# The step from 32 to 64 rows of a block inverse on 64-column weights, and a new order of the instructions

## The chip, the cores and the metric

One core of one Trainium2 chip. The metric is the device time of one execution of the kernel in microseconds (us); lower is better. The kernel before takes 2718.01 us, the median of three runs (2717.71, 2718.01 and 2719.68).

## The reference

One decoder layer on 2048 tokens of width 1024. Its first half joins a gated DeltaNet mixer (8 heads of width 128, chunks of 64 tokens) with a cross-attention of 4 heads to 256 memory rows; an output projection, a layer norm, a squared-ReLU MLP (1024 to 4096 to 1024) and a second layer norm follow. What the change touches is the triangular solve of the DeltaNet: for every head and every chunk

```
a_mat = eye(64) + strict_lower((k * beta) @ k.T * decay)
u = solve(a_mat, v * beta)
w = solve(a_mat, k * beta * exp(g))
```

The kernel takes chunks of 128 tokens for the 64 of the reference, which gives the same result; it computes the inverse of each 128x128 `a_mat` and multiplies by it.

## The kernel before, in words

**Blocks and heads.** The tokens are taken in four blocks of 512. In the mixer of a block a loop of ten steps (`mixer`) runs three stages of a software pipeline over the heads: `dense` projects q, k and v of head t (24 matmuls each), `gdn_a` builds the decayed products of head t-1, inverts them (`invert`) and scales the rest, `gdn_b` runs the recurrence of head t-2 over its four 128-token tiles. Gate projections (`az`), memory projections and attention (`amq`, `sps`, `pmT`, `pmo`) fill further places of the steps. After two blocks come the output projection (`out_seven`, tile `ao`) and the two MLP products (`ff1`, `ff2`; `fA` to `fC` and `f2A` to `f2C`), each as seven products of half-size operands. All of it happens twice.

**Two kinds of matmuls.** Large products run on operands split into a high and a low part of type float32r; each matmul on these is one record of the profile, with 128 weight columns and mostly 512 moving ones. This text calls them f32r. The inverse, the recurrence, some of the key products (`pkq`, four heads), the gates' first product (`aab`) and the transposes have float32 operands; a matmul on these makes two records of the profile and a transpose one. This text calls them f32. The profile prints f32 for both, so they are told apart by the tile's name.

**The inverse** (`invert`, lines 889 to 1007) works on one head's four 128-token tiles at a time; each product on TensorE takes them two by two (index c). Blocks of 16 rows are solved on VectorE. Then three steps double the size, 16 to 32, 32 to 64 and 64 to 128, each with the same form: product `pq` of a part of the lower triangle, copy from PSUM, product `pp` with the inverse so far, copy from PSUM with the sign turned. Each product is two matmuls (c = 0, 1), so four records. The middle step is this:

```
pq = bank("pq", ...)[:, :64]                       # L32: 128 weight columns, ZP: 32 moving
for c in range(2): nc.tensor.matmul(pq[:, c], L32[:, c], ZP[:, c] ...)
nc.scalar.copy(out=Q[:, 64:P] ..., in_=pq)
for c in range(2): nc.tensor.matmul(pp[:, c], X32[:, c], Q[:, 64 + c * 32:...])
```

There are 4 blocks x 8 heads = 32 inversions. The tiles XB, LB, L32, X32, X64, LP and Q stand in four slots (`INV`, `inverse_tiles`) that are set to zero once for every two blocks; ZP lies in the first half of `Lq`, the negated result and its transpose in the second half and in the first again.

**The order.** Nothing is issued while the Python code runs. `Recorder` notes every instruction with an estimate of its time (`cost`); `issue` then plays a list schedule: whenever an engine is free, it takes, of the instructions whose operands are ready by the estimate, the one with the lowest priority number. That number is the place in the program, shifted by a table (`PLACE`, read by `spot`) keyed by block, step and stage: B for `gdn_b`, A for `gdn_a`, D for `dense`, Z for the gates, F for a panel of `ff1`, X and W for the operands of `out_seven`, and so on. The order covers all engines, with SP's DMA issues among them, and is written out with fixed semaphores; on the chip each engine works through its own list in that order. All instructions are issued at line 431 (`o.fn`), which is why the profile shows one line; groups are told apart by tiles. In the schedule of before a change in the number of weight columns can be given a cost (`SWITCH`), which is 0.

`gate_rows` is of use for the prediction: it multiplies 32-column weights (`abw`) on 512 moving columns, float32, into the four quarters of `aab`'s partitions. `gates` holds the transpose `pgt`, whose result has 32 partitions.

Of the kernel before, what the change touches and what calls it, by code (L numbers as in the profile page):

```python
# [14 lines left out]
P = 128  # L15
# [20 lines left out]
DRAIN, SWITCH = {"DVE": 90, "ACT": 100, "POOL": 98}, 0  # L36
# [148 lines left out]
class Op:  # L185
    __slots__ = ("i", "eng", "fn", "args", "kw", "dur", "extra", "succ", "npred", "ready", "start", "end", "load", "last",
                 "bufs", "turns", "prio", "quads", "cols", "late", "lhs")
# [21 lines left out]
class Recorder:  # L209
# [66 lines left out]
    @staticmethod  # L276
    def cost(o, name, wr, rd, args, kw):
        e = o.eng
        shapes = [r.shape for r in wr] + [r.shape for r in rd]
        n = max([_prod(s[1:]) for s in shapes] or [1])  # L280
        if e == "PE":
            rhs = kw.get("rhs", args[2])
            mo, n = _prod(args[1].shape[1:]), _prod(rhs.shape[1:])
            f32 = name == "transpose" or isinstance(rhs, Ref) and rhs.buf.dtype == F32
            o.load, o.cols, o.lhs = 4 + 0.84 * mo, mo, args[1].buf if isinstance(args[1], Ref) else None
            o.last = 2.4 + 0.8334 * n if f32 else 13.4 + 0.4167 * n
            if name == "transpose":
                return o.last
            if f32 and mo == 32 and n == 512:
                return (o.last + max(o.last, o.load)) / 4  # L290
            if f32:
                return o.last + max(o.last, o.load)
            return o.last
        psum = any(r.buf.psum for r in rd + wr)
        if e == "SP":
            n = _prod(wr[0].shape if wr else rd[0].shape)
            o.extra = 1700 + n * 4 / 300.0
            o.late = 2000 if rd and any(s[0] == "partition_broadcast" for s in rd[0].steps) else 300
            return 450
        scal = [v for v in args[2:] if not isinstance(v, (int, float))] if name.startswith("tensor_scalar") else []  # L300
        scal += [v for k, v in kw.items() if k in ("scalar", "scalar1", "scale", "bias") and not isinstance(v, (int, float))]
        if e == "ACT":
            n = _prod((wr[0]).shape[1:])
            return 52 + 0.833 * n + (0 if psum else 42) + 93 * len(scal) + ((305 if scal else 198) if "accum_out" in kw else 0)
        if e == "DVE":
            slow = 30 if name in ("transpose", "stream_shuffle") else 0
            fast = not psum and not any(r.perm() for r in rd + wr) and name in ("tensor_copy", "tensor_scalar_mul", "tensor_scalar_add", "tensor_scalar_max",
                                         "memset")
            return 68 + slow + (0.52 if fast else 1.042) * n + 62 * len(scal) + (7 * n if name == "reciprocal" else 0)
        if name == "memset":  # L310
            return 40 + 0.83 * n
        if kw.get("op") == ALU.pow:
            return 460 + 165 * n
        if name == "tensor_copy":
            return 120 + 0.83 * n
        if name == "affine_select":
            return 125 + 0.9 * n
        return 150 + (2.1 if n < 64 else 2.8) * n if name == "tensor_tensor" else 296 + 3.34 * n

    def issue(self):  # L320
# [7 lines left out]
        quads, cols = {e: {} for e in DRAIN}, P  # L328
# [42 lines left out]
        while True:  # L371
# [3 lines left out]
            for e in engs:  # L375
                if avail[e]:
# [10 lines left out]
            while soon[e] and soon[e][0][0] <= t:  # L387
                r, i, o = heapq.heappop(soon[e])
                heapq.heappush(avail[e], (o.prio, i, o))
            o = heapq.heappop(avail[e])[2]  # L390
            if e == "PE":
                if o.cols != cols:
                    t += SWITCH
                    cols = o.cols
                t = max(t, fed + o.load)
                fed = t + o.dur - o.last
            if e in DRAIN:
# [4 lines left out]
            o.start, o.end = t, t + o.dur  # L402
# [45 lines left out]
def hybrid_layer(  # L448
# [91 lines left out]
    for h in range(H):  # L540
# [7 lines left out]
    INV = (("XB", (2, P)), ("LB", (2, P)), ("L32", (2, P)), ("X32", (2, P)), ("X64", (2, P)),  # L548
           ("LP", (2, P)), ("Q", (2 * P,)))

    def inverse_tiles():
        d = {}
        for i in range(0, len(INV), 2):
            t = slot("inv", "iv")
            nc.gpsimd.memset(t, 0.0)
            for j, (n, shape) in enumerate(INV[i:i + 2]):
                v = t[:, j * 2 * P:(j + 1) * 2 * P]
                d[n] = v if len(shape) == 1 else v.rearrange("p (u f) -> p u f", u=2)
# [330 lines left out]
    def invert(L, par):  # L889
# [8 lines left out]
        for p in range(2):  # L898
            rows = slice(64 * p + 32, 64 * p + 64)
            nc.gpsimd.tensor_copy(L32[rows, :, 64 * p:64 * p + 32].part((0, p)), L[rows, 0:2, 64 * p:64 * p + 32])  # L900
            nc.vector.tensor_copy(L32[64 * p:64 * p + 32, :, 64 * p + 32:64 * p + 64].part((1, p)),
# [28 lines left out]
        XB, LB, X32, X64, Q = (inv[n] for n in ("XB", "LB", "X32", "X64", "Q"))  # L930
# [13 lines left out]
        Q16 = Q[:, :64].rearrange("p (u f) -> p u f", u=2)  # L944
# [4 lines left out]
        for c in range(2):  # L949
            nc.tensor.matmul(pp[:, c * 32:(c + 1) * 32], XB[:, c, :W], Q[:, c * 32:(c + 1) * 32].part(0, 3),  # L950
# [5 lines left out]
        ZP = Lq.rearrange("p c f -> p (c f)")[:, :64].rearrange("p (c f) -> p c f", c=2)  # L956
        Z = small("Z32", [P, NC, 32], 2)
        for p in range(2):
            odd = slice(64 * p + 32, 64 * p + 64)
            nc.vector.tensor_copy(ZP[64 * p:64 * p + 32].part(2 * p + 1), ZT[odd, 2:4])  # L960
            nc.scalar.copy(out=ZP[odd].part(2 * p), in_=ZT[odd, 0:2])
        nc.vector.transpose(Z.rearrange("p c f -> p (c f)"), ZT.rearrange("p c f -> p (c f)"))
        for p in range(2):
            for u in range(2):
                q = quads[2 * p + u]
                nc.vector.tensor_copy(X32[q, :, q].part((u, p)), Z[64 * p:64 * p + 32, 2 * u:2 * u + 2])
# [7 lines left out]
        pq = bank("pq", "ga%d" % par)[:, :64].rearrange("p (c f) -> p c f", c=2)  # L974
        for c in range(2):
            nc.tensor.matmul(pq[:, c], L32[:, c], ZP[:, c].part(0, 1, 2, 3), start=True, stop=True)
        nc.scalar.copy(out=Q[:, 64:P].rearrange("p (c f) -> p c f", c=2).part(1), in_=pq)
        pb = bank("pp", "ga%d" % par)[:, :64]
        pp = pb.rearrange("p (c f) -> p c f", c=2)
        for c in range(2):  # L980
            nc.tensor.matmul(pp[:, c], X32[:, c], Q[:, 64 + c * 32:64 + (c + 1) * 32].part(1), start=True, stop=True)
        Nf = Lq.rearrange("p c f -> p (c f)")[:, 64:]
        nc.scalar.activation(Nf, pb, AF.Copy, scale=-1.0)
        tr = Lq.rearrange("p c f -> p (c f)")[:64, :64]
        nc.vector.transpose(tr, Nf[:64])
        N3 = Nf.rearrange("p (c f) -> p c f", c=2)
        for p in (1, 0):
            o = Y3[64 * p:64 * p + 32, :, 64 * p + 32:64 * p + 64]
            nc.vector.tensor_copy(o[:, 2:4], N3[quads[2 * p + 1]])
            nc.scalar.copy(out=o[:, 0:2], in_=N3[quads[2 * p]])  # L990
        tr = tr.rearrange("p (c f) -> p c f", c=2)
        for u in range(2):
            nc.vector.tensor_copy(X64[quads[2 * u + 1], :, quads[2 * u]].part((u, 2)), tr[quads[u]])
# [7 lines left out]
        nc.scalar.copy(out=Q[:, P:].rearrange("p (c f) -> p c f", c=2).part(2), in_=pq)  # L1001
        pp = bank("pp", "ga%d" % par)[:, :P].rearrange("p (c f) -> p c f", c=2)
        for c in range(2):
            nc.tensor.matmul(pp[:, c], X64[:, c], Q[:, P + c * 64:P + (c + 1) * 64].part(2), start=True, stop=True)
# [912 lines left out]
```

## Time and profile before

| | before |
|---|---|
| median of 3 runs | 2718.01 us (2717.71 to 2719.68) |
| span of the profiled execution | 2718.7 us |
| TensorE busy | 2702.6 us (99%), 13625 records |
| VectorE busy | 2097.3 us (77%) |
| ScalarE busy | 1627.0 us (60%) |
| GpSimd busy | 403.6 us (15%) |
| mean granted TensorE clock | 0.999 |

The profile gives no time of the profiled execution apart from its span, from the first to the last instruction; it lies 0.7 us above the median and within the three runs. PE stands for matmuls, PEld for weight loads. Records of matmuls overlap, since each lasts until its last result is written, so what one costs is read from the start of one to the start of the next. In the timeline neighbouring instructions of one kind are merged into one row: start, length to the end of the last, engine, tiles, weight rows*columns, moving shape, number of records.

### The profile page before, as it was taken

What the parts mean: (1) busy time and instruction counts of PE and PEld (TensorE: products, weight loads), DVE (VectorE), ACT (ScalarE), POOL (GpSimd) and SP (SyncE); (2) the same over time, 40 slices, a digit from 0 to 9 for tenths busy, and PEclk for the clock granted to TensorE, in tenths of its full rate; (3) what the DMA queues carried; (4) which work ended last, traced back from release to release, by engine and by line L of the source; (5) the groups of instructions that cost most, each with busy time, mean ns of one, the idle gap of its engine ahead of it and who ended that gap; (6) DMA issues with size and microseconds to landing.
All of it is one profiled execution on the core that took longest, in us unless ns stands there. A gap on an engine that the chain in (4) does not pass through costs nothing.

```text
span 2718.7 us, 42521 instructions
## 1 busy us (share of the span) xinstructions
PE 2702.6 (99%) x13625; PEld 2264.0 (83%) x13625; DVE 2097.3 (77%) x5652; ACT 1627.0 (60%) x4106; POOL 403.6 (15%) x1031
## 2 busy tenths in 40 slices
PE   9999999999999999999999999999999999999998
PEld 7888888888888888888888888888888888888887
DVE  7999989998877776755767888788878666567575
ACT  7778767776575555334446776677656655554342
POOL 4233223331000000000022231332201000000000
PEclk9999999999999999999999999999999999999999
DMA  8766649867788888766663445444678644486673
GB/s 315 253 232 210 213 170 321 293 240 261 278 315 286 297 294 298 264 212 197 231 226 136 171 137 186 156 152 157 226 260 295 220 164 141 158 283 221 214 238 112
DMA packets 209072, 613.81 MB, mean 226 GB/s; under 512 B 24112, under 2 KB 32720, under 8 KB 188880
## 3 DMA queue, kind: packets, MB, share of 16 engines
q1 hardware_dynamic: 208416, 611.04, 64.7%
q8 instruction: 108, 1.77, 0.3%
q14 instruction: 116, 0.95, 0.1%
q10 hardware_dynamic: 432, 0.05, 0.0%
HBM read 436.35 MB, written 174.65 MB: 225 GB/s over the span
## 4 chain that ended last, share of the span: by engine, by line
PE 94%; DVE 2%; ACT 2%; DMA 1%; POOL 1%; issue 0%; SPq 0%; DVEq 0%; ACTq 0%; POOLq 0%
PE f2A L431 13%; PE fA L431 13%; PE ao L431 8%; PE fC L431 6%; PE f2C L431 6%; PE az L431 6%; PE aq L431 6%; PE av L431 6%; PE ak L431 6%; PE amq L431 3%; PE fB L431 3%; PE f2B L431 3%; PE pc L431 3%; PE po L431 2%; PE pkq L431 2%; PE pq L431 1%
## 5 line engine op out<-in xcount | busy, mean ns | idle before, releaser
L431 DVE TENSOR_TENSOR whl<-wraw,whl 128x512 fp32r<-128x512 f32 (+2 forms) x294 | 256.5, 883 | 109.8 <-ACT whl L431 107.9
L431 ACT CAST whl<-wraw 128x512 fp32r<-128x512 f32 (+2 forms) x294 | 226.4, 781 | 164.4 <-PE fC L431 54.5
L431 PE MATMUL fA<-B,whl 128*128 128x512 f32 x1152 | 279.1, 389 | 0.0
L431 PE MATMUL f2A<-whl,X 128*128 128x512 f32 x1152 | 262.1, 389 | 0.0
L431 ACT CAST X<-X 128x1024 fp32r<-128x1024 f32 x118 | 124.0, 1052 | 223.3 <-DMA X<-xsc 183.3
L431 PEld LDWEIGHTS fA<-B,whl 128*128 128x128 f32 x1152 | 216.2, 188 | 45.1
L431 PEld LDWEIGHTS f2A<-whl,X 128*128 128x128 f32 x1152 | 216.2, 188 | 44.9
L431 DVE TENSOR_TENSOR X<-X,X 128x1024 fp32r<-128x1024 f32 x118 | 143.8, 1221 | 126.0 <-ACT X L431 125.9
L431 PE MATMUL az<-T,whl 128*128 128x512 f32 x768 | 218.5, 406 | 0.0
L431 PE MATMUL aq<-T,whl 128*128 128x512 f32 x768 | 215.6, 406 | 1.7 <-DVE whl L431 0.8
L431 PE MATMUL ak<-T,whl 128*128 128x512 f32 x768 | 214.8, 407 | 0.1
L431 PE MATMUL av<-T,whl 128*128 128x512 f32 x768 | 209.1, 402 | 0.0
L431 PE MATMUL fC<-B,whl 128*128 128x512 f32 x768 | 192.3, 389 | 0.0
L431 PE MATMUL f2C<-whl,X 128*128 128x512 f32 x768 | 174.7, 389 | 0.0
L431 PEld LDWEIGHTS fC<-B,whl 128*128 128x128 f32 x768 | 144.1, 188 | 30.0
L431 PEld LDWEIGHTS f2C<-whl,X 128*128 128x128 f32 x768 | 144.1, 188 | 29.9
L431 PEld LDWEIGHTS aq<-T,whl 128*128 128x128 f32 x768 | 137.5, 189 | 27.4 <-DVE T L431 2.0
L431 PEld LDWEIGHTS av<-T,whl 128*128 128x128 f32 x768 | 138.5, 189 | 24.3
L431 PEld LDWEIGHTS ak<-T,whl 128*128 128x128 f32 x768 | 135.8, 189 | 22.3 <-ACT whl L431 0.4
L431 PEld LDWEIGHTS az<-T,whl 128*128 128x128 f32 x768 | 136.4, 189 | 21.2
L431 POOL TENSOR_SCALAR ve<-mv 128x1 f32<-128x1 f32 x34 | 15.3, 451 | 912.2 <-DVE mv L431 906.0
L431 PE MATMUL ao<-whl,X 128*128 128x512 f32 x528 | 136.8, 401 | 0.0
(294 smaller groups left out, 6292.2 us busy)
## 6 DMA issues: line engine op xcount, KB each, us to landing
whl<-wsc SPq DMA_DIRECT2D x108, 1024.0 KB, 4.9
wraw<-in_w_ff_dram SPq DMA_DIRECT2D x106, 512.0 KB, 4.3
X<-xsc SPq DMA_DIRECT2D x96, 512.0 KB, 4.1
wsc<-whl SPq DMA_DIRECT2D x36, 1024.0 KB, 6.4
whl<-tsc SPq DMA_DIRECT2D x64, 512.0 KB, 4.8
xsc<-hB SPq DMA_DIRECT2D x96, 256.0 KB, 2.5
xo<-cat SPq DMA_DIRECT2D x80, 256.0 KB, 4.1
wraw<-in_w_in_dram SPq DMA_DIRECT2D x35, 512.0 KB, 6.5
```

The source lines that it names most:

```text
L431: o.fn(*[res(a) for a in o.args], **{k: res(v) for k, v in o.kw.items()})
```

## The change

Part one is the middle step of the inverse. The blocks of the weights of `pq` and `pp` are moved together, so that they have 64 columns where they had 128 (L32 and X32 become 2 x 64), and the moving operands have 64 columns where they had 32 (new tiles Z64 and Q64 with zeros in half their places). The result stands on 64 partitions. Its sign is turned once, 32 rows of it are transposed, and one copy on each of VectorE and ScalarE puts it into Y where there were two. Z64, Q64, N and NT have places of their own in the four slots of the inverse's tiles.

Part two is the order. Each matmul is marked `wide` if it is f32, and TensorE gets two heaps of ready work. After f32 work it stays with f32 work if that has a priority number below that of the f32r work plus 200 (`STAY`); after fewer than five f32r matmuls it goes back only to f32 work whose number is lower by more than 300 (`LEAVE`, `RUN`); otherwise the lower number wins. The schedule's estimate adds 5 ns on entering f32 work and up to 8 ns to each of the first ten f32r matmuls behind it. The table PLACE is replaced by a longer one.

```diff
-DRAIN, SWITCH = {"DVE": 90, "ACT": 100, "POOL": 98}, 0
+DRAIN = {"DVE": 90, "ACT": 100, "POOL": 98}
+INTO, AFTER = 5, (8, 4, 6, 6, 0, 4, 5.5, 1.5, 4, 2.5)
+STAY, LEAVE, RUN = 200, 300, 4
...
 PLACE = {
-    ('w',): 140, (0, 0, 'H'): -305, (0, 1, 'D'): -225, (0, 1, 'H'): -435, (0, 1, 'Y'): -145, (0, 1, 'Z'): -165,
...
+    (None,): -90, ('w',): 135, (0, 0, 'D'): 255, (0, 0, 'F'): -420, (0, 0, 'H'): -300, (0, 1, 'A'): 185,
...
             f32 = name == "transpose" or isinstance(rhs, Ref) and rhs.buf.dtype == F32
+            o.wide = f32 or not isinstance(rhs, Ref)
...
-                heapq.heappush(avail[e], (o.prio, i, o))
-            o = heapq.heappop(avail[e])[2]
+                heapq.heappush(wide if e == "PE" and o.wide else avail[e], (o.prio, i, o))
+            heap = avail[e]
+            if e == "PE" and wide:
+                if not heap:
+                    heap = wide
+                elif was:
+                    heap = wide if wide[0][0] < heap[0][0] + STAY else heap
+                elif run < RUN:
+                    heap = wide if wide[0][0] < heap[0][0] - LEAVE else heap
+                else:
+                    heap = wide if wide[0][:2] < heap[0][:2] else heap
+            o = heapq.heappop(heap)[2]
...
-    INV = (("XB", (2, P)), ("LB", (2, P)), ("L32", (2, P)), ("X32", (2, P)), ("X64", (2, P)),
-           ("LP", (2, P)), ("Q", (2 * P,)))
+    INV = ((("XB", (2, P)), ("LB", (2, P))), (("X64", (2, P)), ("LP", (2, P))),
+           (("L32", (2, 64)), ("X32", (2, 64)), ("Z64", (2, 64)), ("Q64", (2, 64))),
+           (("Q16", (64,)), ("Q", (P,)), ("N", (NC, 32)), ("NT", (NC, 32))))
...
-        pq = bank("pq", "ga%d" % par)[:, :64].rearrange("p (c f) -> p c f", c=2)
+        pq = bank("pq", "ga%d" % par)[:64, :P].rearrange("p (c f) -> p c f", c=2)
         for c in range(2):
             nc.tensor.matmul(pq[:, c], L32[:, c], ZP[:, c].part(0, 1, 2, 3), start=True, stop=True)
-        nc.scalar.copy(out=Q[:, 64:P].rearrange("p (c f) -> p c f", c=2).part(1), in_=pq)
-        pb = bank("pp", "ga%d" % par)[:, :64]
-        pp = pb.rearrange("p (c f) -> p c f", c=2)
+        for u in range(2):
+            nc.scalar.copy(out=QP[64 * u:64 * u + 64, :, 32 * u:32 * u + 32].part(u), in_=pq[:, :, 32 * u:32 * u + 32])
+        pp = bank("pp", "ga%d" % par)[:64, :P]
         for c in range(2):
-            nc.tensor.matmul(pp[:, c], X32[:, c], Q[:, 64 + c * 32:64 + (c + 1) * 32].part(1), start=True, stop=True)
-        Nf = Lq.rearrange("p c f -> p (c f)")[:, 64:]
-        nc.scalar.activation(Nf, pb, AF.Copy, scale=-1.0)
...
+            nc.tensor.matmul(pp[:, c * 64:(c + 1) * 64], X32[:, c], QP[:, c].part(0, 1), start=True, stop=True)
+        nc.scalar.activation(N3[:64].rearrange("p (u c) f -> p u c f", u=2), pp.rearrange("p (c u f) -> p u c f", c=2, u=2),
+                             AF.Copy, scale=-1.0)
+        nc.vector.transpose(NT[:32].rearrange("p c f -> p (c f)"), N3[:32].rearrange("p c f -> p (c f)"))
+        nc.vector.tensor_copy(Y3[64:96, :, 96:], N3[32:64])
+        nc.scalar.copy(out=Y3[:32, :, 32:64], in_=N3[:32])
```

## Rows read from the trace of the kernel before

**Rows 1.** The page's busy times, and the core's span with its granted clock

```profile
PE 2702.6 (99%) x13625; PEld 2264.0 (83%) x13625; DVE 2097.3 (77%) x5652; ACT 1627.0 (60%) x4106; POOL 403.6 (15%) x1031
...
core 0: 2718.7 us, clock 0.999
```

**Rows 2.** Who PE waited for: total us, times, longest

```profile
PE pt L431 <- ACT st L431: 1.4, 2, 0.9
...
PE pt L431 <- ACT y L431: 0.2, 1, 0.2
```

**Rows 3.** A window of the first MLP: length, then busy us and records per engine

```profile
780.00:1320.00 540.00, 540.00 (x2384) 447.11 (x2383) 381.45 (x526) 267.29 (x387) 6.88 (x14) 1.00 0.78 266
```

**Rows 4.** PE's groups by shape: the middle step's first product

```profile
L431 PE MATMUL pq<-Lq,inv 128*128 128x32 f32 x128 | 17.1, 255 | 0.3 <-POOL inv L431 0.3
```

**Rows 5.** PEld's groups by shape: busy us, mean ns of one load

```profile
L431 PEld LDWEIGHTS pp<-inv 128*128 128x128 f32 x256 | 36.8, 190 | 5.9 <-issue 0.9 <-ACT inv L431 0.8 <-POOL halo L431 0.2
...
L431 PEld LDWEIGHTS aab<-xj,abw 128*32 128x32 f32 x64 | 1.5, 108 | 3.1 <-issue 2.7 <-DVE Xc L431 0.4
```

**Rows 6.** PE's timeline in mixers: f32 work between stretches of f32r work

```profile
413.00 0.53 PE L431 MATMUL pp<-inv 128*128 128x32 f32 x4
413.36 3.24 PE L431 MATMUL ak<-T,whl 128*128 128x512 f32 x13
416.44 0.55 PE L431 MATMUL pq<-YP,inv 128*128 128x64 f32 x4
...
564.03 0.56 PE L431 MATMUL pq<-YP,inv 128*128 128x64 f32 x4
564.40 1.18 PE L431 MATMUL ak<-T,whl 128*128 128x512 f32 x4
565.41 0.55 PE L431 MATMUL pp<-inv 128*128 128x64 f32 x4
...
577.20 0.27 PE L431 MATMUL pmT<-ident,pr 128*128 128x128 f32 x1
577.23 0.48 PE L431 MATMUL av<-T,whl 128*128 128x512 f32 x1
577.55 0.38 PE L431 MATMUL pkq<-ck 128*128 128x128 f32 x2
577.76 0.39 PE L431 MATMUL pkq<-cq,ck 128*128 128x128 f32 x2
```

**Rows 7.** The first and the last f32 stretch of PE's timeline

```profile
1.19 4.64 PE L431 MATMUL warm<-ones 128*128 128x128 f32 x20 [1.19 <-POOL mhalf L518]
...
2110.02 0.60 PE L431 MATMUL pt<-ident,y 128*128 128x128 f32 x4
```

**Rows 8.** PE's timeline around matmuls and a transpose on 32-column weights

```profile
303.15 1.06 PE L431 MATMUL aab<-xj,abw 128*32 128x512 f32 x8
304.15 0.73 PE L431 MATMUL sps<-mkv,mq 128*128 128x256 f32 x4
...
1340.28 0.39 PE L431 MATMUL f2A<-whl,xl 128*128 128x512 f32 x1
1340.59 1.92 PE L431 MATMUL aab<-xj,abw 128*32 128x512 f32 x16
1342.45 0.74 PE L431 MATMUL f2A<-whl,xh 128*128 128x512 f32 x2
1343.03 0.40 PE L431 MATMUL f2A<-whl,xl 128*128 128x512 f32 x1
...
1367.11 0.39 PE L431 MATMUL f2A<-whl,xl 128*128 128x512 f32 x1
1367.34 0.27 PE L431 MATMUL pgt<-ident,gc 128*32 128x128 f32 x1
1367.36 0.71 PE L431 MATMUL f2A<-whl,xh 128*128 128x512 f32 x2
1367.91 0.40 PE L431 MATMUL f2A<-whl,xl 128*128 128x512 f32 x1
```

More of the change, by code (lines that the diff above doesn't have):

```diff
@@ L186 @@
     __slots__ = ("i", "eng", "fn", "args", "kw", "dur", "extra", "succ", "npred", "ready", "start", "end", "load", "last",
-                 "bufs", "turns", "prio", "quads", "cols", "late", "lhs")
+                 "bufs", "turns", "prio", "quads", "cols", "late", "lhs", "wide")
 PLACE = {
[15 rows of a table removed]
[35 rows of a table added]
 }
@@ L327, in issue @@
         dma = [0.0]
-        quads, cols = {e: {} for e in DRAIN}, P
+        quads = {e: {} for e in DRAIN}
+        wide, was, run = [], False, len(AFTER)
         slots = {k: [0.0] * v[0].bufs for k, v in self.tags.items()}
@@ L375, in issue @@
             for e in engs:
-                if avail[e]:
+                if avail[e] or e == "PE" and wide:
                     t = free[e]
@@ L388, in issue @@
                 r, i, o = heapq.heappop(soon[e])
-                heapq.heappush(avail[e], (o.prio, i, o))
-            o = heapq.heappop(avail[e])[2]
+                heapq.heappush(wide if e == "PE" and o.wide else avail[e], (o.prio, i, o))
[10 more added lines that the diff above has]
+            o = heapq.heappop(heap)[2]
+            took = o.dur
             if e == "PE":
-                if o.cols != cols:
-                    t += SWITCH
-                    cols = o.cols
                 t = max(t, fed + o.load)
                 fed = t + o.dur - o.last
+                if o.wide:
+                    took += 0 if was else INTO
+                else:
+                    run = 0 if was else run + 1
+                    took += AFTER[run] if run < len(AFTER) else 0
+                was = o.wide
             if e in DRAIN:
@@ L401, in issue @@
                 at.update(o.quads)
-            o.start, o.end = t, t + o.dur
+            o.start, o.end = t, t + took
             free[e] = o.end
@@ L547, in hybrid_layer @@
     nc.gpsimd.memset(halo, 0.0)
-    INV = (("XB", (2, P)), ("LB", (2, P)), ("L32", (2, P)), ("X32", (2, P)), ("X64", (2, P)),
-           ("LP", (2, P)), ("Q", (2 * P,)))
+    INV = ((("XB", (2, P)), ("LB", (2, P))), (("X64", (2, P)), ("LP", (2, P))),
+           (("L32", (2, 64)), ("X32", (2, 64)), ("Z64", (2, 64)), ("Q64", (2, 64))),
+           (("Q16", (64,)), ("Q", (P,)), ("N", (NC, 32)), ("NT", (NC, 32))))
     def inverse_tiles():
         d = {}
-        for i in range(0, len(INV), 2):
+        for names in INV:
             t = slot("inv", "iv")
             nc.gpsimd.memset(t, 0.0)
-            for j, (n, shape) in enumerate(INV[i:i + 2]):
-                v = t[:, j * 2 * P:(j + 1) * 2 * P]
-                d[n] = v if len(shape) == 1 else v.rearrange("p (u f) -> p u f", u=2)
+            at = 0
+            for n, shape in names:
+                v = t[:, at:at + _prod(shape)]
+                at += _prod(shape)
+                d[n] = v if len(shape) == 1 else v.rearrange("p (u f) -> p u f", u=shape[0])
         return d
@@ L899, in invert @@
             rows = slice(64 * p + 32, 64 * p + 64)
-            nc.gpsimd.tensor_copy(L32[rows, :, 64 * p:64 * p + 32].part((0, p)), L[rows, 0:2, 64 * p:64 * p + 32])
-            nc.vector.tensor_copy(L32[64 * p:64 * p + 32, :, 64 * p + 32:64 * p + 64].part((1, p)),
+            nc.gpsimd.tensor_copy(L32[rows, :, 32 * p:32 * p + 32].part((0, p)), L[rows, 0:2, 64 * p:64 * p + 32])
+            nc.vector.tensor_copy(L32[64 * p:64 * p + 32, :, 32 * p:32 * p + 32].part((1, p)),
                                   L[rows, 2:4, 64 * p:64 * p + 32])
@@ L929, in invert @@
         nc.vector.transpose(ZT.rearrange("p c f -> p (c f)"), Z.rearrange("p c f -> p (c f)"))
-        XB, LB, X32, X64, Q = (inv[n] for n in ("XB", "LB", "X32", "X64", "Q"))
+        XB, LB, X32, X64, Q, ZP, QP, N3, NT = (inv[n] for n in ("XB", "LB", "X32", "X64", "Q", "Z64", "Q64", "N", "NT"))
         Y = slot("Y", "s0")
@@ L943, in invert @@
             nc.tensor.matmul(pq[:, c], LB[:, c], ZT[:, c:NC:2, 16:32], start=True, stop=True)
-        Q16 = Q[:, :64].rearrange("p (u f) -> p u f", u=2)
+        Q16 = inv["Q16"].rearrange("p (u f) -> p u f", u=2)
         nc.scalar.activation(Q16[:, :, 0:16].part(0), pq[:, :, 0:16], AF.Copy, scale=half[:, 0:1])
@@ L949, in invert @@
         for c in range(2):
-            nc.tensor.matmul(pp[:, c * 32:(c + 1) * 32], XB[:, c, :W], Q[:, c * 32:(c + 1) * 32].part(0, 3),
+            nc.tensor.matmul(pp[:, c * 32:(c + 1) * 32], XB[:, c, :W], Q16[:, c].part(0, 3),
                              start=True, stop=True)
@@ L953, in invert @@
         nc.vector.tensor_tensor(out=zt, in0=zt, in1=pp.rearrange("p (u k f) -> p u k f", u=2, k=2), op=ALU.subtract)
-        ZP = Lq.rearrange("p c f -> p (c f)")[:, :64].rearrange("p (c f) -> p c f", c=2)
         Z = small("Z32", [P, NC, 32], 2)
@@ L959, in invert @@
             odd = slice(64 * p + 32, 64 * p + 64)
-            nc.vector.tensor_copy(ZP[64 * p:64 * p + 32].part(2 * p + 1), ZT[odd, 2:4])
-            nc.scalar.copy(out=ZP[odd].part(2 * p), in_=ZT[odd, 0:2])
+            nc.vector.tensor_copy(ZP[64 * p:64 * p + 32, :, 32:].part(2 * p + 1), ZT[odd, 2:4])
+            nc.scalar.copy(out=ZP[odd, :, :32].part(2 * p), in_=ZT[odd, 0:2])
         nc.vector.transpose(Z.rearrange("p c f -> p (c f)"), ZT.rearrange("p c f -> p (c f)"))
@@ L964, in invert @@
             for u in range(2):
-                q = quads[2 * p + u]
-                nc.vector.tensor_copy(X32[q, :, q].part((u, p)), Z[64 * p:64 * p + 32, 2 * u:2 * u + 2])
+                nc.vector.tensor_copy(X32[quads[2 * u + p], :, 32 * p:32 * p + 32].part((u, p)),
+                                      Z[64 * p:64 * p + 32, 2 * u:2 * u + 2])
         for p in range(2):
@@ L972, in invert @@
             nc.scalar.copy(out=Y3[r, :, r], in_=ZT[r])
-        pq = bank("pq", "ga%d" % par)[:, :64].rearrange("p (c f) -> p c f", c=2)
+        pq = bank("pq", "ga%d" % par)[:64, :P].rearrange("p (c f) -> p c f", c=2)
         for c in range(2):
             nc.tensor.matmul(pq[:, c], L32[:, c], ZP[:, c].part(0, 1, 2, 3), start=True, stop=True)
-        nc.scalar.copy(out=Q[:, 64:P].rearrange("p (c f) -> p c f", c=2).part(1), in_=pq)
-        pb = bank("pp", "ga%d" % par)[:, :64]
-        pp = pb.rearrange("p (c f) -> p c f", c=2)
+        for u in range(2):
+            nc.scalar.copy(out=QP[64 * u:64 * u + 64, :, 32 * u:32 * u + 32].part(u), in_=pq[:, :, 32 * u:32 * u + 32])
+        pp = bank("pp", "ga%d" % par)[:64, :P]
         for c in range(2):
-            nc.tensor.matmul(pp[:, c], X32[:, c], Q[:, 64 + c * 32:64 + (c + 1) * 32].part(1), start=True, stop=True)
-        Nf = Lq.rearrange("p c f -> p (c f)")[:, 64:]
-        nc.scalar.activation(Nf, pb, AF.Copy, scale=-1.0)
[L984 to L991, printed above, removed]
+            nc.tensor.matmul(pp[:, c * 64:(c + 1) * 64], X32[:, c], QP[:, c].part(0, 1), start=True, stop=True)
[4 more added lines that the diff above has]
+        nc.scalar.copy(out=Y3[:32, :, 32:64], in_=N3[:32])
         for u in range(2):
-            nc.vector.tensor_copy(X64[quads[2 * u + 1], :, quads[2 * u]].part((u, 2)), tr[quads[u]])
+            nc.vector.tensor_copy(X64[quads[2 * u + 1], :, quads[2 * u]].part((u, 2)), NT[:32, 2 * u:2 * u + 2])
         YP = small("YP", [P, 2, 64], 1)
@@ L1000, in invert @@
             nc.tensor.matmul(pq[:, c], LP[:, c], YP[:, c], start=True, stop=True)
-        nc.scalar.copy(out=Q[:, P:].rearrange("p (c f) -> p c f", c=2).part(2), in_=pq)
+        nc.scalar.copy(out=Q.rearrange("p (c f) -> p c f", c=2), in_=pq)
         pp = bank("pp", "ga%d" % par)[:, :P].rearrange("p (c f) -> p c f", c=2)
         for c in range(2):
-            nc.tensor.matmul(pp[:, c], X64[:, c], Q[:, P + c * 64:P + (c + 1) * 64].part(2), start=True, stop=True)
+            nc.tensor.matmul(pp[:, c], X64[:, c], Q[:, c * 64:(c + 1) * 64], start=True, stop=True)
         nc.vector.tensor_scalar_mul(Y3[:64, 2:4, 64:], pp[64:], -1.0)
```

48 rows, old and new, of the table PLACE are left out of this document.

## The prediction

> **What bounds the kernel now.** I read the page's busy times and the span first, then PE's waits, then its groups by shape, and last its timeline. The matmul engine PE is busy for 99% of 2718.7 us at a granted clock of 0.999, the vector and scalar engines for 77% and 60% [rows 1]. Then who PE waited for: the eleven groups of that view sum to 6.4 us, the largest being 1.4 us and the last 0.2 [rows 2]. So the time is what PE's instructions cost one behind the other, and an edit counts for what it does to that.
>
> PE's costs come from starts, not from lengths. In the MLP, where only f32r work runs, 2384 matmuls take 540 us, 0.2265 us each [rows 3]. An f32 record on 128x128 costs 0.11: two of `pkq` start 0.21 us before the next pair [rows 6]. Where the two kinds alternate, a trip to f32 and back costs a little more than its parts. With one f32r matmul between, from `pmT` to `pkq`, it is 0.35 for 0.11 + 0.227: 0.013 over. With four, 1.38 for 0.44 + 0.906: 0.034 over. With thirteen, 3.44 for 0.44 + 2.945: 0.055 over [rows 6]. So a trip costs 0.013 at least and some 0.05 at most; it grows with the f32r stretch behind it and then stops growing. I counted the f32 stretches over the whole timeline: 750, the first and last of which are shown [rows 7]. The f32r stretches behind them have 1, 2, 3 or 4 matmuls 107, 70, 112 and 129 times (418 stretches, 1099 matmuls), 5 to 19 in 291 (2249 matmuls), 20 or more in 41, and one is the last.
>
> **Part one, the inverse's middle step.** Each product is 128 records [rows 4], and the second product makes as many, so 32 inversions x 2 products = 64 visits of four records each, apart from one another, because an eviction from PSUM lies between `pq` and `pp`. Now a record costs 0.11, and what sets this is the weight load, since 32 moving columns and 64 cost alike (both groups of four in the stretches above fit 0.44). A load lasts 190 ns for 128 columns and 108 for 32 [rows 5]: 0.85 ns a column, so 64 columns save 55 ns and leave 0.055. Sixty-four moving columns stream in half of the 0.11 of 128, so the stream does not bind either. A visit thus saves 4 x 0.055 = 0.22 us; over 64 visits 14.1 us.
>
> Against it stands what narrower weights cost at the edges of a visit, which no row shows for 64 columns. The nearest rows are `aab`, float32 matmuls on 32 columns. Eight of them take 1.00 us and sixteen 1.86, so two more groups of four take 0.86, 0.43 a group: four run at once on quarters of the array [rows 8]. Around sixteen of them, from the f2A start at 1340.28 to that at 1343.03, lie 2.75 us; three f32r matmuls (0.68) and four groups (1.72) explain 2.40. The other 0.35 us are the visit's edges: PE starts the first `aab` 0.31 after a matmul of 0.227, and the rest goes at the far side [rows 8]. At the other end is `pgt`, a transpose with 32 columns: from 1367.11 to 1367.91, 0.80 us for 3 x 0.227 + 0.11 = 0.79, so nothing beyond the ordinary trip [rows 8].
>
> I take the `aab` price. Like the new products it is a plain float32 matmul whose weights fill a part of the columns; `pgt` differs in kind. From 0.35 I subtract the ordinary trip (0.017, paid before too) and add 0.027 for a first load of 64 columns instead of 32 that no matmul covers (32 x 0.85 ns). That is 0.36 a visit against 0.22 saved: +0.14, times 64: **+9.0 us**. By `pgt` it would be -14.1. I keep both ends.
>
> The Trainium skill has a rule that speaks against this change: the page "TensorEngine Tiling (Array Packing)", section Key Properties, says that a change of tiling mode drains TensorE, and its section Performance Considerations counts weights of at most 64 columns as 2x column tiling. Its Restrictions set transposes of float32 apart from column tiling, which would explain `pgt`. By that rule the sum is the +9.0, without it -14.1; the trace agrees for 32 columns and is silent on 64.
>
> On the other engines an inversion loses one VectorE copy and keeps four ScalarE instructions between `pq` and the next step (one copy of `pq` becomes two, two copies into Y become one). Slots and their memsets stay four. These lie beside PE, at 77% and 60% [rows 1], and I cost them at nothing; if that cover were gone, the copy added on the chain from `pq` to `pp` would delay `pp`, while f32r work fills PE. Z64, Q64 and N exist once, so the next inversion's writes wait for this one's readers, a whole pipeline step earlier: nothing.
>
> **Part two, the order.** It adds no instruction; all lists are drawn anew, SP's loads and GpSimd's among them. Its gain can only come from fewer trips and fewer waits. The trips now cost: 418 short stretches at some 0.023 (their mean is 2.6 matmuls) 9.6 us, 291 at 0.04 (mean 7.7) 11.6, 41 at 0.05 2.1, together some 23 us. The new rule asks for at least five f32r matmuls before PE goes back, unless the f32 work is far ahead in priority or no f32r work is ready. If the 1099 short-stretch matmuls came in stretches of seven, there would be 157 at 0.038, 6.0 us: 3.6 saved. If all 3348 came in twenties, 167 at 0.05 are 8.4 of 21.2: 12.8 saved. But fewer trips are longer ones, and a trip is dearer behind a longer stretch, so most of the saving is given back; and the f32 stages are links of chains (in `gdn_b` twelve for a head, in `invert` six) with an eviction between, so many come ready alone. I take -4, nearest to the regrouping that the rule enforces, and -1 for waits, as f32 work that is held back finds its operands there; ends -13 and +5. The +5 is loads or copies arriving late in the new lists, each up to the 0.7 us mean of the longest group of waits [rows 2], seven of them.
>
> **Sum.** 9.0 - 5 = +4.0 us. The profiled execution's span of 2718.7 is 0.7 over the median of 2718.0, within the three runs; I count from the median: **2722 us**, range for this case 2716 to 2727. What a measurement can tell from no change is 0.2%, 5.4 us.
>
> **The rivals.** First, the 64-column products behave like `pgt`: no edge cost. For it: `pgt` is the one other row with few columns, and it is free; `aab` runs on four quarters at once, the new products on one half alone. Against it: `aab` is nearer in kind, and its edges cost the engine time whatever stands around them. 2718.0 - 14.1 - 5 = 2699, range 2694 to 2705. Faster; 0.20.
>
> Second, and on the slower side: the edges cost as `aab` says, and the order does not do what it says. Wherever the chains' stages come ready one at a time, staying with f32 finds nothing to stay with, and the trips merge only on paper. This decides from the point where the stretches number some 700 or more, or are fewer by as much as they are dearer. Then nothing offsets the visits: 2718.0 + 9.0 = 2727; 0.22.
>
> Third, holding f32 work back makes `gdn_b`'s chain late where it is alone, at the end of the second mixer of each pair of blocks, before `out_seven`. Twelve stages of a head, each held for two f32r matmuls more (0.45 us), 5.4 us, at two places: 10.8 on top of +4.0, so 2733; 0.07. That the longest group of waits is 1.4 us now speaks against it [rows 2].
>
> Fourth, the order gets the whole 12.8, with the edges: 2718.0 + 9.0 - 13 = 2714; 0.07.
>
> **How the numbers follow.** The forecast has 0.44, the rivals 0.20, 0.22, 0.07 and 0.07. Slower by over 5.4 us: nearly all of the second, the third, a little of the forecast: 0.29. Faster by as much: the first, a third of the fourth, a little of the forecast: 0.25. The rest, 0.46, is within. The range 2697 to 2728 leaves out the third and the lower part of the first.
>
> **What would show it.** In the changed kernel's timeline the groups of four on 128*64 weights should lie some 0.22 us apart within (0.055 a record) with gaps ahead and behind: the first record over 0.3 us after the last f32r start, and the f32r matmul behind starting or ending some 0.2 late. Loads of 64 columns should last some 135 ns. The stretches should number 450 to 600 for 750, with few of under five f32r matmuls. The first rival is right if the visit's rows fit 0.22 plus an ordinary trip. The prediction is wrong in its second part if the waits of PE grow beyond 6.4 us by several, or if the MLP's 0.2265 no longer holds.

## The result, and the profile after

The changed kernel takes 2726.54 us (median of seven runs, 2725.47 to 2728.47) against 2718.76 for the kernel before, measured beside it (seven runs, 2717.71 to 2719.68). The ratio is 1.003, interval 1.0021 to 1.004: 7.8 us slower, inside the range, 4.5 above the predicted 2722.0. The case that came true is not the forecast but the second rival.

The page of the kernel after, its busy times and span, against [rows 1]:

```profile
PE 2708.8 (99%) x13625; PEld 2254.4 (83%) x13625; DVE 2087.9 (77%) x5620; ACT 1626.3 (60%) x4106; POOL 415.1 (15%) x1031
...
core 0: 2724.2 us, clock 0.999
```

PE is busy 6.2 us longer in a span 5.5 us longer, at the same clock and with as many records; VectorE issues 32 instructions less, the 32 copies taken out. So the time still lies on PE. The run that was traced took 2725.96 us, 1.8 above its span and 0.6 below the median; the ten runs traced below lie 1.7 or 1.8 above their spans as well. By that the traced run of before took some 2720.4 (an estimate), 1.7 above its median (the 0.7 named ahead compares a span with times). So the traces show 5.5 us of the 7.8 that the medians do.

Who PE waited for, kernel after (total us, times, longest), the first three and the last of twelve groups, against [rows 2]:

```profile
PE warm L469 <- POOL mhalf L556: 1.2, 1, 1.2
PE pmo L469 <- DVE pm L469: 0.6, 1, 0.6
PE pg L469 <- DVE gg L469: 0.5, 1, 0.5
...
PE po L469 <- DVE cat L469: 0.2, 1, 0.2
```

They sum to 5.8 us for 6.4: nothing here is 7.8 us late. The MLP is unchanged too, with the same window as [rows 3]:

```profile
780.00:1320.00 540.00, 540.00 (x2384) 447.09 (x2383) 383.34 (x533) 269.62 (x393) 7.58 (x14) 1.00 0.78 267
```

The difference is in the mixers. First the edited products, PE's groups by shape with busy us and mean ns, against [rows 4]:

```profile
L469 PE MATMUL pq<-inv 128*64 128x64 f32 x128 | 14.3, 234 | 0.4 <-ACT inv L469 0.4
L469 PE MATMUL pp<-inv 128*64 128x64 f32 x128 | 14.2, 234 | 0.2 <-DVE inv L469 0.2
```

By this view they are cheaper: 14.3 us for 17.1, 234 ns a record for 255. The view of their weight loads, `pq` of the kernel before first (for `pp` see [rows 5]), shows that something else has come:

```profile
L431 PEld LDWEIGHTS pq<-Lq,inv 128*128 128x128 f32 x128 | 18.6, 190 | 2.6 <-POOL inv L431 0.7
...
L469 PEld LDWEIGHTS pq<-inv 128*64 128x64 f32 x128 | 9.8, 136 | 10.5 <-issue 8.8 <-ACT inv L469 0.8 <-ACT Y L469 0.4
L469 PEld LDWEIGHTS pp<-inv 128*64 128x64 f32 x128 | 9.8, 136 | 9.9 <-issue 3.6 <-ACT joss L469 1.1 <-ACT th L469 0.7
```

A load takes 136 ns for 190, but the weight loader stood idle 10.5 and 9.9 us before these two groups, where the kernel before has 2.6 for `pq`. For `pq` most of that ends with "issue" (8.8), which is no other engine, for `pp` about a third (3.6). What that costs shows in the timeline, one visit with five f32r matmuls to the next, first in the kernel before and then in the one after:

```profile
517.79 0.53 PE L431 MATMUL pq<-Lq,inv 128*128 128x32 f32 x4
518.15 1.40 PE L431 MATMUL ak<-T,whl 128*128 128x512 f32 x5
519.39 0.53 PE L431 MATMUL pp<-inv 128*128 128x32 f32 x4
```

```profile
459.19 1.77 PE L469 MATMUL av<-T,whl 128*128 128x512 f32 x7
460.89 0.45 PE L469 MATMUL pq<-inv 128*64 128x64 f32 x4
461.27 1.43 PE L469 MATMUL av<-T,whl 128*128 128x512 f32 x5
462.62 0.45 PE L469 MATMUL pp<-inv 128*64 128x64 f32 x4
```

From `pq` to `pp` lie 1.60 us before and 1.73 after. The four records are shorter (0.45 for 0.53), yet the f32r work begins 0.38 after the first of them where it was 0.36, and `pp` comes 0.22 after five times 0.2265 from there, where it was 0.11. The last of the seven f32r matmuls starts at 460.57, so the first record of the visit comes 0.32 behind it.

The last f32 stretch stands where it stood [rows 7], 4.6 us later:

```profile
2114.59 0.60 PE L469 MATMUL pt<-ident,y 128*128 128x128 f32 x4
```

The stretches number 700 for 750; 317 of the f32r stretches behind them are still of under five matmuls (1, 2, 3 or 4: 96, 49, 94 and 78 times), where it was 418; 157 have exactly five, where it was 91.

### The profile page after: what moved, and what is told of

It is laid out like the page before. It is cut to its first block, busy times and chain, and to the rows that moved or that the text cites. A ratio compares the mean times of both kernels' runs of the same rounds, so it can differ in the third digit from the quotient of the medians.

```text
span 2724.2 us, 42515 instructions
## 1 busy us (share of the span) xinstructions
PE 2708.8 (99%) x13625; PEld 2254.4 (83%) x13625; DVE 2087.9 (77%) x5620; ACT 1626.3 (60%) x4106; POOL 415.1 (15%) x1031
## 4 chain that ended last, share of the span: by engine, by line
PE 94%; ACT 2%; DVE 1%; POOL 1%; DMA 1%; issue 1%; ACTq 0%; DVEq 0%; SPq 0%; POOLq 0%
PE fA L469 13%; PE f2A L469 13%; PE ao L469 8%; PE av L469 6%; PE f2C L469 6%; PE fC L469 6%; PE ak L469 6%; PE az L469 6%; PE aq L469 6%; PE fB L469 3%; PE f2B L469 3%; PE pc L469 3%; PE amq L469 3%; PE po L469 2%; PE pkq L469 2%; PE pq L469 1%
## 5 line engine op out<-in xcount | busy, mean ns | idle before, releaser
L469 PE MATMUL fA<-B,whl 128*128 128x512 f32 x1152 | 289.4, 389 | 0.0
L469 PE MATMUL az<-T,whl 128*128 128x512 f32 x768 | 231.0, 406 | 0.0
L469 PE MATMUL av<-T,whl 128*128 128x512 f32 x768 | 216.0, 404 | 0.0
L469 PE MATMUL aq<-T,whl 128*128 128x512 f32 x768 | 209.0, 405 | 0.5 <-DVE T L469 0.4
L469 PEld LDWEIGHTS aq<-T,whl 128*128 128x128 f32 x768 | 137.6, 189 | 27.6 <-DVE T L469 1.7
```

What stands on the lines that cost most here:

```text
L469: o.fn(*[res(a) for a in o.args], **{k: res(v) for k, v in o.kw.items()})
```

## The experiments

My theory after the result: the 64-column visits cost some 0.13 us each at their edges, and the order gives nothing for it. Rivals: that the lists drawn anew bring waits, and that the visits are not what costs. A visit is four records, and a change of the inverse also changes every engine's list, so I first changed one part with the list left free, and then held the list.

### One part at a time, lists drawn anew

Three edits were combined. The inverse of either kernel; the scheduler with its table (`cost`, `issue`, `PLACE`) of either kernel; and a new variant of the changed inverse, whose weights have 72 columns where 64 are needed; the readers take the first 64 rows of the result, and the eight columns of zeros are read by nobody:

```diff
-(("L32", (2, 64)), ("X32", (2, 64)), ("Z64", (2, 64)), ("Q64", (2, 64))),
-(("Q16", (64,)), ("Q", (P,)), ...
+(("L32", (2, 72)), ("X32", (2, 72)), ("Z64", (2, 64)), ("Q16", (64,))),
+(("Q64", (2, 64)), ("Q", (P,)), ...
-        pq = bank("pq", "ga%d" % par)[:64, :P]...
+        pq = bank("pq", "ga%d" % par)[:72, :P]...
-        pp = bank("pp", "ga%d" % par)[:64, :P]
+        pp = bank("pp", "ga%d" % par)[:72, :P]
```

**The 64-column inverse with scheduler and table of before:**

> The new inverse with the scheduler and the table of before. Theory (the edges of a visit to 64-column weights cost more than its shorter loads save, +0.13 us for each of 64 visits): 8 us slower than before, about 2727. Rival (the new order costs the time and the visits are free of edges): 14 us faster, about 2705.

Measured: 2745.68 us, ratio 1.0098 (1.0085 to 1.0112).

**The new scheduler and table with the inverse of before:**

> The new scheduler and table with the inverse of before. Theory: the order is worth little, 0 to 3 us faster than before, 2716 to 2719, with some 690 f32 stretches for 750. Rival (the order costs the time): 8 us or more slower than before.

Measured: 2751.35 us, ratio 1.0121 (1.0105 to 1.0136).

**The changed kernel with 72 columns:**

> The changed kernel with 72 weight columns in the middle step, 8 of them zero, whose results are not read. Theory (the weights of 64 columns put the array in another arrangement and those of 72 do not): the edges go, a record costs 0.062 us, a visit 0.25 and an ordinary trip; 0.33 less for each of 64 visits, 21 us faster than the changed kernel, about 2706. Rival (the folding or the 64 moving columns cost the time, whatever the arrangement): within 3 us of the changed kernel, 2724 to 2730.

Measured: 2746.18 us, ratio 1.0102 (1.0089 to 1.0116).

**72 columns with scheduler and table of before:**

> The new inverse on 72 weight columns with the scheduler and the table of before. Theory: 256 records at 0.062 for 0.11 us, 12 us faster than before, about 2707. Rival (folding costs): slower than before.

Measured: 2722.48 us, ratio 1.0015 (1.0006 to 1.0023).

No theory was met: the first and the third fall outside both of their cases, the second and the fourth on the side of their rivals. Three of the four are slower than both kernels by 19 to 33 us, which no sum of the two parts allows. The waits tell why. Rows of PE's waits, first of the 64-column inverse alone, then of the 72 columns in the changed kernel:

```profile
PE pto L431 <- ACT on L431: 4.7, 3, 3.9
PE ao L431 <- DVE whl L431: 3.1, 2, 1.8
```

```profile
PE ptv L469 <- ACT Y L469: 3.3, 8, 0.7
PE ao L469 <- DVE whl L469: 2.4, 5, 0.6
```

Single waits are as long as 3.9 us; by the split used further down, all waits come to 33.2, 49.5, 53.1 and 30.1 us in the four kernels, where they are 18.5 before. I read this so: a list drawn with a table that was made for another program puts work where its operands are late, far from the edit too (`ao` belongs to `out_seven`). A table fitted to the 72 columns, at the end of this section, brings the 53.1 us down to 24.2. By their medians these four runs cannot tell the parts apart. What the split leaves without waits does: some 10 us more than before with 64 columns, no change with the old inverse, and 10 and 9 us less with 72.

### The list held

So the list was written into the kernel: `issue` no longer chooses, but emits every engine's instructions in the order that one of the two kernels has.

```diff
-            o = heapq.heappop(heap)[2]
...
-            out.append(o)
...
+        d.frombytes(zlib.decompress(base64.b85decode(ORDER)))
+        for x in d:
+            at += x
+            out.append(self.ops[at])
```

Where the inverses differ, the four ScalarE and VectorE copies stand where their counterparts stood: for the list of before, the second copy of `pq` right behind the first, and two of the four copies into Y dropped; the reverse for the list of after with the old inverse. In the traces the 13625 records of PE have the same tiles in the same order in all three kernels of a list. With the two kernels themselves this fills a table of three inverses and two lists.

**64 columns, list of before:**

> The list of before, one for one, with the new inverse on 64 columns put into its places: the inverse alone, without a new list. Theory: 64 visits at 0.58 for 0.452 us, 8.2 us slower than before, about 2727. Rival (the 27 us of the inverse alone with its newly drawn list are the inverse's own): about 2745.

Measured: 2724.56 us, ratio 1.0022 (1.0014 to 1.0031).

**72 columns, list of before:**

> The list of before, one for one, with the new inverse on 72 columns in its places. Theory: 64 visits at 0.311 for 0.452 us, 9 us faster than before, about 2709.5. Rival (the new list was needed for any gain): within 3 us of before.

Measured: 2715.60 us, ratio 0.999 (0.9981 to 0.9999).

**The old inverse, list of after:**

> The changed kernel's list, one for one, with the inverse of before in its places: the new order alone. Theory: the changed kernel less 8.2 us of visits, about 2718, so the new order is worth 0 to 2 us against before. Rival (my forecast's order term): 5 us faster than before, about 2713.5.

Measured: 2723.99 us, ratio 1.002 (1.0011 to 1.0029).

**72 columns, list of after:**

> The changed kernel's own list of instructions, one for one, with 72 weight columns for 64 in the middle step. Theory (edges of the 64-column visits): a visit falls from 0.58 us to 0.31, as the two traces measured it, 64 of them: 17 us faster than the changed kernel, about 2709. Rival (a drawn list fits only the durations it was drawn with, so that PE waits elsewhere and the gain is lost): 2720 or more.

Measured: 2719.41 us, ratio 1.0004 (0.9995 to 1.0013).

By the medians only the first of these comes near its theory; the other three lie 6 to 10 us above theirs. To read them I split every trace after its first 16 us in two. For each matmul record I took the time from the end of the record before to its own end, and compared it with what is usual for its kind, its predecessor's kind and its place in the stretch (the lower third over all these traces). What lies over 25 ns above the usual counts as wait; it holds small delays too that the view of PE's waits leaves out. The rest is what the order costs if nothing is late. With other classes and other limits for what is usual, the differences between two rows below move by up to some 1 us.

| inverse | list | median us | without waits | waits |
|---|---|---|---|---|
| 128 columns | before (kernel before) | 2718.76 | 2668.9 | 18.5 |
| 64 columns | before | 2724.56 | 2676.7 | 14.2 |
| 72 columns | before | 2715.60 | 2659.5 | 22.7 |
| 128 columns | after | 2723.99 | 2667.5 | 23.3 |
| 64 columns | after (kernel after) | 2726.54 | 2675.6 | 17.1 |
| 72 columns | after | 2719.41 | 2658.5 | 27.5 |

**The visits.** Without waits the 64 columns cost 7.8 us on the one list and 8.1 on the other, 0.12 to 0.13 for each of the 64 visits. The 72 columns save 9.4 and 9.0. Eight columns of zeros more are worth 17 us by this count, and 9.0 and 7.1 by the medians. That excludes that the wider moving operand, the other copies or the new tiles cost the time, since 64 and 72 columns share all of these. The timeline shows it at the same place as above, on 64 columns and then on 72, both with the list of before:

```profile
518.58 0.45 PE L713 MATMUL pq<-inv 128*64 128x64 f32 x4
518.95 1.43 PE L713 MATMUL ak<-T,whl 128*128 128x512 f32 x5
520.31 0.45 PE L713 MATMUL pp<-inv 128*64 128x64 f32 x4
```

```profile
516.39 0.41 PE L713 MATMUL pq<-inv 128*72 128x64 f32 x4
516.61 1.40 PE L713 MATMUL ak<-T,whl 128*128 128x512 f32 x5
517.85 0.41 PE L713 MATMUL pp<-inv 128*72 128x64 f32 x4
```

From `pq` to `pp` 1.73 and 1.46 us, with 1.60 for 128 columns. With 72 the f32r work begins 0.22 after the first record; with 64 it takes 0.37. By the medians over such visits, set against 72 columns, some 0.14 us are lost up to the second record and some 0.14 behind the last. And most of the weight loader's idle time is gone with 72 columns; its row with the list of after:

```profile
L751 PEld LDWEIGHTS pq<-inv 128*72 128x72 f32 x128 | 13.0, 143 | 4.1 <-ACT inv L751 0.9
```

4.1 us of idle time for the 10.5 above, and "issue" is no longer among its ends. So entering and leaving 64-column work makes PE's own sequence stand still, and 72-column work does not.

**The order.** Without waits the new list saves 1.4, 1.1 and 1.0 us, on 128, 64 and 72 columns; that is hardly more than the split can tell (0 to 2 with other limits). By the medians it costs 5.2, 2.0 and 3.8: the waits grow by 4.8, 2.9 and 4.8. One row of the weight loads' waits shows where some of them are: `ptv`, the transposes of v behind an inversion, go into the PSUM bank that the inversion's last product stood in, and wait until ScalarE has copied that into Y. First with the old inverse on the list of after, then with 72 columns on it:

```profile
PEld ptv L752 <- ACT Y L752: 5.7, 13, 0.9
```

```profile
PEld ptv L751 <- ACT Y L751: 6.5, 14, 1.0
```

In the kernel after, the row is shorter:

```profile
PEld ptv L469 <- ACT Y L469: 2.8, 8, 0.6
```

**The waits follow PE's work.** On either list the dearer inverse has the smaller waits: 27.5, 23.3 and 17.1 us for 72, 128 and 64 columns on the list of after. Between the 128 columns and the others, 34.3 us of differences without waits stand beside 18.9 of opposite ones in the waits, roughly half. That other engines are then simply ready in time is argued from the row above, not shown for all of it.

### A table for 72 columns

On the list of before, 72 columns beat both kernels, if by little. Would a table made for them gain more? Theory: it brings the waits down to those of before. Rival: the estimate by which a table is made does not see these waits, so they stay. One table was drawn up with the new rule and one without, each fitted under the schedule's own estimate (the diff is that of the second; the first has another table and keeps the rule's three numbers):

```diff
-STAY, LEAVE, RUN = 200, 300, 4
+STAY, LEAVE, RUN = 0, 0, 0
...
-    (None,): -90, ('w',): 135, (0, 0, 'D'): 255, (0, 0, 'F'): -420, (0, 0, 'H'): -300, (0, 1, 'A'): 185,
...
+    (): -245, (None,): 20, (0, 0, 'D'): 20, (0, 0, 'F'): 50, (0, 0, 'H'): -385, (0, 0, 'n'): -120,
...
```

**With the rule:**

> The changed kernel with 72 columns and a table PLACE of its own, fitted to the durations of 72 columns. Theory (the edges are gone, and what the runs on borrowed lists lost again was the misfit of the list): matmuls, trips and edges as with 72 columns on the other two lists, 10 us less than before, and waits of PE like those of the two fitted lists, 17 to 19 us: about 2708. Rival (whatever PE saves turns into waits, as on the borrowed lists, because the other engines are late): waits of 23 to 28 us, 2713 to 2719.

Measured: 2715.36 us, ratio 0.9988 (0.9979 to 0.9997); without waits 2658.6, waits 24.2; 688 stretches, 315 of them short.

**Without the rule:**

> The same with STAY, LEAVE and RUN at 0, so that the lower priority number always wins, and again a table of its own. Theory (keeping f32 work together saves little, since a trip is dearer behind a longer f32r stretch): within 2 us of the run with the rule, some 720 stretches for 690. Rival (the rule is worth what I forecast, 5 us): 2712 or more, 5 us slower than the run with the rule.

Measured: 2718.75 us, ratio 1.0000 (0.9991 to 1.0009); without waits 2658.8, waits 27.6; 723 stretches, 437 short.

The waits stay, as the rival says; its reason, that the estimate does not see them, was not tried by itself. With the new table the row from above is as long as ever:

```profile
PEld ptv L470 <- ACT Y L470: 6.9, 14, 0.9
```

122 short stretches fewer are worth 0.2 us without waits, which is nothing that the split can tell. The 3.4 us between the two medians lie between the theory's 2 and the rival's 5; they are the waits of two tables, each drawn up once, and say little of the rule. Both fastest versions (2715.60 and 2715.36) are 3 us below the kernel before. Which engine's cost the estimate has wrong, so that ScalarE's copies come late, stays open; it wasn't tried.

## Why the prediction was right, and where it was not

**What bounds the kernel** held in the main: PE at 99%, and the MLP's 540 us to the hundredth. That an edit counts for what it does to PE's sequence held for half: I took the 6.4 us of PE's view for all that PE waits; by the split the kernel before has 18.5, and an edit moves them. The first step behind it, the **price of a visit**, had the right end and nearly the right size: +9.0 forecast, +7.8 and +8.1 measured without waits. It was right for the reason given: `aab`, the plain float32 matmul on few columns, was the row to go by, and not `pgt`. Loads of 64 columns take 136 ns where 135 were forecast, the second to the fourth record of a visit start 0.058 apart where 0.055 was forecast, and the first came 0.32 after the last f32r start where "over 0.3" was named. The first rival, no edges, is out.

Both parts of that price were a little large. I had all four records of a visit save 0.055. The visits of 72 and 112 columns (112 are those of `pp` in the step from 16 to 32) say three: from the end of the last f32r record before it to the end of the first behind it, less the 0.2265 of that one, a visit costs about 0.452 us with 128 columns, 0.411 with 112 and 0.311 with 72. Three records at 16 columns and 0.85 ns are 0.041, and three at 47 ns (190 less 143) are 0.141, which are the two differences. The first record follows an f32r matmul and does not wait for its load alone. So by this estimate 64 columns save 3 x 0.054 = 0.16, would leave 0.29, and measure 0.580: the edges are 0.29, not 0.36. The saving was 0.06 too large and the edges 0.07; that the two cancel in the +9.0 is luck.

The rule of the Trainium skill, page "TensorEngine Tiling (Array Packing)", sections Key Properties and Performance Considerations, by which weights of at most 64 columns are column tiling and a change of mode drains TensorE, agrees with the trace: 64 columns lose 0.29 us a visit, 72 nothing. The trace shows the loss, not a drain itself.

**The step that failed is the order.** I took -4 for fewer trips and -1 for fewer waits. The trips gave -1.1 to -1.4. Their price fits, and their number was wrong: I expected 450 to 600 stretches with few short ones, and there are 700 with 317 short. At 0.023 for 317, 0.038 for 336 (their mean is 7.2 f32r matmuls, and the prediction has 0.038 for seven) and 0.05 for 47 they cost 22.4 us for 23.3 before: 0.9 saved, near the 1.0 to 1.4 measured. With the 0.04 that the prediction has for the class of 5 to 19 it is 0.2; both agree with the split. I had let the rule collect the matmuls of all short stretches into sevens; but it only holds f32 work back until the fifth f32r matmul, and the stage that has been held then comes alone, as it did before; the 157 stretches of exactly five fit that. The second rival named that, from 700 stretches on.

The waits went the other way than I took them: on an equal inverse the new list adds 2.9 to 4.8 us of them, within the +5 that I kept as an end. In the kernel after this is hidden, because the dearer visits take as much away: 18.5 to 17.1 us in all. So the prediction's test, that PE's waits grow beyond 6.4, was not met, though the cause it was meant for is there. I had also put the change of the other engines' waits under part one at nothing; it is -4.3 on the list of before and -6.2 on that of after.

In sum, from traces: +7.8 (visits, list of before), -4.3 (waits they hide), -1.1 (trips), +2.9 (waits of the new list) = +5.3 for the spans' +5.5, and the 2.3 us to the medians' 7.8 are the two traced runs, 1.7 above and 0.6 below their medians. The second rival's 2727, from +9.0 and nothing, is close because terms that it does not have cancel; so far that is luck. The forecast's range held by 0.5 us.

The third rival, a late chain at the end of the second mixer, did not come: no group of PE's waits in the kernel after but the start-up one is above 0.6 us. The fourth, the whole 12.8 from the order, is excluded by its 1.4.

## What to carry to other kernels

Where short groups of float32 matmuls on few weight columns alternate with full-width f32r work, keep their weights above 64 columns if the loads are to get shorter (72 and 112 were measured): padding 64 to 72 was worth 17 us of PE's time and 7 to 9 of the kernel's here, over 64 visits. Count how often an ordering rule can really act before multiplying by a price, since chained stages come ready one at a time whatever the rule wants. In a kernel with a written-out order, compare two versions of a part on the same list, and split the time into what the order costs and what is late, or a change of the list will hide the part: drawing it anew moved the time by up to 33 us.

## What the runs showed that I had not expected

The edge of a 64-column visit is paid on both sides and is absent eight columns higher: 0.580 us for four records with 64 columns, 0.311 with 72, while the load differs by 7 ns (136 and 143). PE's view of its waits shows none of it, and the groups by shape show the dearer products as cheaper (234 ns for 255); it is to be seen in the weight loads' idle time ended by "issue" (8.8 us for `pq` on 64 columns) and in starts read from the timeline.

About half of a change in PE's work, and up to three quarters, came back with the other sign as waits, though the other engines are busy only 77% and 60% of the time: on the list of after, 9.0 us saved by 72 columns brought 4.2 us more waits, and 8.1 lost by 64 columns took 6.2 away; by the medians the two give 4.6 and 2.6 for 9.0 and 8.1. I had counted that cover as free.
